# A hybrid decoder layer on one core: rows of the normed, turned input 2064 bytes apart in place of 2048

## The chip, the cores and the metric

The kernel runs on one core of one Trainium2 chip. The metric is the device time of one execution in microseconds; lower is better. The kernel before was run three times.

## What is computed

One decoder layer on 256 tokens of 1024 channels, in float32. Two token mixers (an RWKV-7 recurrence and a block-sparse attention, which at this length is plain causal attention) work on one normed input, and a gated MLP with a short convolution follows. Cut to the parts that matter here:

```python
h = rms_norm(x, norm1_g[l])
proj = h @ w_in[l]                       # 1024 -> 1824 + 1536 + 2048 columns
z_rwkv = proj[..., :RWKV_IN]
z_moba = proj[..., RWKV_IN:RWKV_IN + MOBA_IN]
gate_pre = proj[..., RWKV_IN + MOBA_IN:]
...                                      # y_a = RWKV-7 of z_rwkv, y_b = attention of z_moba
u_a = y_a @ w_branch_a[l]
u_b = y_b @ w_branch_b[l]
x = x + (g_a * u_a + g_b * u_b) @ w_out[l]
h2 = rms_norm(x, norm2_g[l])
x = x + conv_ffn(h2, w_ffn_up[l], ffn_conv_w[l], ffn_conv_b[l], w_ffn_down[l])
```

```python
u = h @ w_up                             # 1024 -> 2 * 2816
a, b = u[..., :D_FF], u[..., D_FF:]
a = causal_depthwise_conv3(a) + conv_b
return (gelu(a) * b) @ w_down
```

## The kernel before

**Numbers in two halves.** Each float32 operand of a large matmul is split into a high half, rounded to the matmul's input type (fp32r), and a low half, the rest. A product is then three matmuls: high by high, low by high, high by low. Weights come from HBM in pieces of 128 partitions by 1024 floats (`raw`); ACT makes the high half `whi` (L238) and DVE the low half `wlo` (L248). `raw` has four buffers, `whi` four, `wlo` three, all of 4096 bytes in a partition. Their refill is triggered by the matmuls that use them up, in `weights()`.

**The tile that the change touches.** `hx` holds the input of the layer's first projections, normed and turned so that channels lie on partitions: 128 partitions, 8 rows k (one for each 128 channels), and in each row the 256 tokens of the high half (`hh`) and behind them the 256 of the low half (`hl`). A row is 512 floats, 2048 bytes, and rows follow one another without a gap, so the tile is 16384 bytes in a partition. It is declared twice under one tag and has one place: first for the projections of the token mixers (L335), then again for the MLP's input (L1103).

```python
hx = cst.tile([128, 8, 2, S], F32R, name="hx", tag="hx")
hh, hl = hx[:, :, 0], hx[:, :, 1]
```

It is written row by row: ACT scales a turned piece out of PSUM into `hh[:, k]` (L393 in the first round, L1118 in the second), and DVE puts what is left into `hl[:, k]` (L396, L1119). Every read takes one row k or part of it; none spans rows.

**Who reads it.** Four places on TensorE, each an accumulation over k:

- `first` (L431) and `wst` (L278, L280, L283): weights are the stationary side, 128 columns; a half row of 256 tokens streams past. `wst` with `hx` makes the projections to r, k, v and the gates. With the outputs of the two mixers (`yah`, `yal`, `ybh`, `ybl`, each a tile of its own of four rows of 1024 bytes) the same lines make the branch projections.
- `xst` (L299, L300, L303): 128 tokens of a row of `hx` are the stationary side, and 512 columns of weights stream past; this makes q, k and v of the attention. With `mh` and `ml`, tiles of their own, the same lines make the output projection.
- `up` (L1160, L1163): weights are stationary. L1160 streams a whole row, both halves at once, 512 wide; L1163 streams the high half against `wlo`, 256 wide. The inner part is this:

```python
for m in range(2):
    ms = slice(m * 128, m * 128 + 128)
    for k in range(4):
        pe.matmul(ps_[m], wh[:, k, ms], hx[:, k0 + k].rearrange("p a s -> p (a s)"),
                  start=k0 + k == 0, stop=False, skip_group_check=True)
    for k in range(4):
        pe.matmul(ps_[m][:, 0:S], wl[:, k, ms], hh[:, k0 + k], start=False,
                  stop=k0 + k == 7, skip_group_check=True)
```

It runs for two k0 and two m, 22 times in all: 88 groups of four wide and four narrow matmuls. The down projection (L1178, L1180, L1182) streams `whi` or `wlo`, 512 wide, against the MLP's inner tile `hb`, and doesn't touch `hx`.

**The order of the work.** The first steps are in an order written by hand. From there to the branch projections, Python generators (a recurrent chain, the attention, a group norm, and `bulk` with the projections) are interleaved by costs and latencies that they hand out, and after that the code runs straight on: output projection, second norm, then eleven rounds of up projection, convolution, GELU and, one round later, down projection. Instructions keep the order in which the code issues them.

**Where tiles lie.** The pool `cst`, which holds `hx` and the constants, comes first in a partition; `hx` begins at byte 29760. The mixers' outputs and a few more tiles of `cst` follow it, then `raw`, `whi` and `wlo`, then all working tiles.

Of the kernel before, what the change touches and what calls it, by code (L numbers as in the profile page):

```python
# [9 lines left out]
F32 = mybir.dt.float32  # L10
F32R = mybir.dt.float32r
# [7 lines left out]
S = 256  # L19
# [17 lines left out]
def body(tc, x, positions, norm1_g, w_in, rwkv_mu, w_decay_up, decay_bias, w_aaa_up,  # L37
# [5 lines left out]
    with ctx:  # L43
        cst = ctx.enter_context(tc.tile_pool(name="cst", bufs=1))
# [24 lines left out]
        def acc(name="acc"):  # L69
            return ps.tile([128, 512], F32, name=name, tag="acc", bufs=3)  # L70
# [261 lines left out]
                queue += [wd[:, 2 * j - 2:2 * j - 1, :], wd[:, 2 * j - 1:2 * j, :]]  # L332
        queue += [wd[:, 20:21, :], wd[:, 21:22, :]]

        hx = cst.tile([128, 8, 2, S], F32R, name="hx", tag="hx")  # L335
        hh, hl = hx[:, :, 0], hx[:, :, 1]

        def first_steps():
# [116 lines left out]
        with tc.manual_schedule(engines={E.PE, E.Activation, E.DVE, E.Pool}):  # L455
            p = first_steps()
# [24 lines left out]
        p = acc()  # L481
# [618 lines left out]


        mh, ml = mhl
        hx = cst.tile([128, 8, 2, S], F32R, name="hx", tag="hx")  # L1103
        hh, hl = hx[:, :, 0], hx[:, :, 1]
        ss = sb.tile([128, 2, 2], F32, name="ss2")
        rs = sb.tile([128, 2], F32, name="rs2")
# [165 lines left out]
```

## Time and profile before

| what | value |
|---|---|
| median of three runs | 413.82 us (413.51 to 414.05) |
| profiled execution, span from first to last instruction | 411.9 us |
| difference between the two | 1.9 us |
| TensorE busy in the span | 404.6 us (98%) |
| VectorE (DVE), ScalarE (ACT), GpSimd (POOL) busy | 322.2, 230.8, 38.3 us |
| mean DMA rate | 172 GB/s |
| mean granted TensorE clock | 1.000 |

The profiled execution has no time of its own beside its span. PE stands for TensorE's matmuls, PEld for its weight loads. A row of a group names the line, the engine, the operation, the tile written and the tiles read, then partitions and elements. A matmul's duration runs from its first read to its modelled end in PSUM, so durations of successive matmuls overlap; the distance from start to start is shorter.

### The profile page before, as it was taken

What the parts mean: (1) busy time and instruction counts of PE and PEld (TensorE: products, weight loads), DVE (VectorE), ACT (ScalarE), POOL (GpSimd) and SP (SyncE); (2) the same over time, 40 slices, a digit from 0 to 9 for tenths busy, and PEclk for the clock granted to TensorE, in tenths of its full rate; (3) what the DMA queues carried; (4) which work ended last, traced back from release to release, by engine and by line L of the source; (5) the groups of instructions that cost most, each with busy time, mean ns of one, the idle gap of its engine ahead of it and who ended that gap; (6) DMA issues with size and microseconds to landing.
All of it is one profiled execution on the core that took longest, in us unless ns stands there. A gap on an engine that the chain in (4) does not pass through costs nothing.

```text
span 411.9 us, 8111 instructions
## 1 busy us (share of the span) xinstructions
PE 404.6 (98%) x3199; PEld 355.6 (86%) x3199; DVE 322.2 (78%) x559; ACT 230.8 (56%) x384; POOL 38.3 (9%) x62
## 2 busy tenths in 40 slices
PE   6999999999999999999999999999999999999996
PEld 3999989888899998999988888888888888888885
DVE  2888999869557876678974898979779678797784
ACT  5799645465444765453653884646446455464450
POOL 8910070000210010120000000000000000000000
PEclk9999999999999999999999999999999999999999
DMA  8955565663483352466564555765665666656612
GB/s 247 314 190 154 156 179 157 163 171 105 95 226 94 104 155 68 146 202 198 175 197 147 160 199 183 225 202 176 199 193 171 199 200 198 200 168 199 198 53 102
DMA packets 61765, 70.72 MB, mean 172 GB/s; under 512 B 8349, under 2 KB 52195, under 8 KB 61728
## 3 DMA queue, kind: packets, MB, share of 16 engines
q1 hardware_dynamic: 60768, 69.41, 56.3%
q0 software_dynamic: 944, 0.80, 0.9%
q8 instruction: 25, 0.41, 0.4%
q14 instruction: 12, 0.10, 0.1%
q10 hardware_dynamic: 16, 0.00, 0.0%
HBM read 68.76 MB, written 1.44 MB: 170 GB/s over the span
## 4 chain that ended last, share of the span: by engine, by line
PE 89%; DVE 4%; ACT 3%; DMA 1%; issue 1%; SPq 0%; POOL 0%; ACTq 0%
PE acc L1160 15%; PE acc L1163 7%; PE acc L278 7%; PE acc L283 7%; PE acc L280 7%; PE at L1160 5%; PE acc L299 5%; PE f L1182 4%; PE acc L303 4%; PE f L1180 4%; PE acc L300 4%; PE f L1178 4%; PE at L1163 2%; ACT sc L970 2%; DMA x<-in_x_dram 1%
## 5 line engine op out<-in xcount | busy, mean ns | idle before, releaser
L238 ACT CAST whi<-raw 128x1024 fp32r<-128x1024 f32 x120 | 125.8, 1051 | 113.6 <-PE acc L1160 26.2
L248 DVE TENSOR_TENSOR wlo<-raw,whi 128x1024 fp32r<-128x1024 f32 x120 | 145.7, 1218 | 41.8 <-PE acc L1163 12.9
L1160 PE MATMUL acc<-hx,whi 128*128 128x512 f32 x264 | 72.4, 395 | 0.0
L278 PE MATMUL acc<-hx,whi 128*128 128x256 f32 x232 | 58.2, 287 | 0.0
L280 PE MATMUL acc<-hx,whi 128*128 128x256 f32 x232 | 56.0, 278 | 0.0
L1160 PEld LDWEIGHTS acc<-hx,whi 128*128 128x128 f32 x264 | 45.3, 188 | 6.3
L1163 PEld LDWEIGHTS acc<-hx,wlo 128*128 128x128 f32 x264 | 40.2, 188 | 6.1
L278 PEld LDWEIGHTS acc<-hx,whi 128*128 128x128 f32 x232 | 43.6, 188 | 1.6 <-issue 0.7
L280 PEld LDWEIGHTS acc<-hx,whi 128*128 128x128 f32 x232 | 43.7, 188 | 0.1
L1163 PE MATMUL acc<-hx,wlo 128*128 128x256 f32 x264 | 41.3, 278 | 0.0
L283 PE MATMUL acc<-hx,wlo 128*128 128x256 f32 x232 | 35.9, 277 | 0.0
L1182 PE MATMUL f<-wlo,hb 128*128 128x512 f32 x80 | 31.3, 391 | 0.0
L1180 PE MATMUL f<-whi,hb 128*128 128x512 f32 x80 | 31.2, 390 | 0.0
L1178 PE MATMUL f<-whi,hb 128*128 128x512 f32 x80 | 31.2, 390 | 0.0
L283 PEld LDWEIGHTS acc<-hx,wlo 128*128 128x128 f32 x232 | 30.7, 188 | 0.3 <-issue 0.3
L1160 PE MATMUL at<-hx,whi 128*128 128x512 f32 x88 | 24.0, 394 | 0.0
L1168 DVE TENSOR_REDUCE an<-acc 128x256 f32<-128x512 f32 x22 | 15.0, 689 | 6.5 <-PE acc L1163 5.6
L299 PE MATMUL acc<-whi,hx 128*128 128x512 f32 x48 | 19.3, 403 | 0.0
L300 PE MATMUL acc<-whi,hx 128*128 128x512 f32 x48 | 18.8, 391 | 0.0
L1182 PEld LDWEIGHTS f<-wlo,hb 128*128 128x128 f32 x80 | 15.0, 188 | 3.5 <-DVE wlo L248 0.4
L1178 PEld LDWEIGHTS f<-whi,hb 128*128 128x128 f32 x80 | 15.0, 188 | 2.8
L1180 PEld LDWEIGHTS f<-whi,hb 128*128 128x128 f32 x80 | 15.0, 188 | 2.8
(311 smaller groups left out, 700.4 us busy)
## 6 DMA issues: line engine op xcount, KB each, us to landing
raw<-in_w_ffn_up_dram SPq DMA_DIRECT2D x44, 512.0 KB, 4.3
raw<-in_w_in_dram SPq DMA_DIRECT2D x38, 512.0 KB, 4.5
raw<-in_w_ffn_down_dram SPq DMA_DIRECT2D x22, 512.0 KB, 3.3
raw<-in_w_out_dram SPq DMA_DIRECT2D x8, 512.0 KB, 4.3
x<-in_x_dram SPq DMA_DIRECT2D x8, 256.0 KB, 5.2
early<-in_w_in_dram SPq DMA_DIRECT2D x4, 512.0 KB, 9.8
raw<-in_w_branch_b_dram SPq DMA_DIRECT2D x4, 512.0 KB, 3.6
raw<-in_w_branch_a_dram SPq DMA_DIRECT2D x4, 512.0 KB, 4.1
```

The lines of the kernel that those rows point to most:

```text
L238: act.copy(hi[:, :k * c], raw[:, :k * c])
L248: eng.tensor_tensor(lo[:, :n], raw[:, :n], hi[:, :n].bitcast(F32), op=OP.subtract)
L278: pe.matmul(om, wh[:, k, ms], xh[:, k0 + k], start=k0 + k + m == 0, stop=False, skip_group_check=True)
L280: pe.matmul(om, wh[:, k, ms], xl[:, k0 + k], start=False, stop=False, skip_group_check=True)
L283: pe.matmul(om, wl[:, k, ms], xh[:, k0 + k], start=False, stop=k0 + k == nk - 1 and m == n - 1, skip_group_check=True)
L299: pe.matmul(ps_[t], xh[:, K, ts], wh[:, k], start=K == 0, stop=False)
L300: pe.matmul(ps_[t], xl[:, K, ts], wh[:, k], start=False, stop=False)
L1160: pe.matmul(ps_[m], wh[:, k, ms], hx[:, k0 + k].rearrange("p a s -> p (a s)"), start=k0 + k == 0, stop=False, skip_group_check=True)
L1163: pe.matmul(ps_[m][:, 0:S], wl[:, k, ms], hh[:, k0 + k], start=False, stop=k0 + k == 7, skip_group_check=True)
L1178: pe.matmul(fin[f], hb[:, 0, i, ts], wh[:, 0, cs], start=st, stop=False, skip_group_check=f == 3)
L1180: pe.matmul(fin[f], hb[:, 1, i, ts], wh[:, 0, cs], start=False, stop=False, skip_group_check=f == 3)
L1182: pe.matmul(fin[f], hb[:, 0, i, ts], wl[:, 0, cs], start=False, stop=False, skip_group_check=f == 3)
```

## The change

Both declarations of `hx` get rows of 516 floats in place of 512, of which the first 512 are used as before. A row is then 2064 bytes from the next, and the tile is 16512 bytes. Behind it, in the same pool, a tile of 96 floats is declared that nothing reads or writes: 384 bytes. So everything that lies behind `hx` in a partition lies 512 bytes further on. The code that uses `hh`, `hl` and `hx` is as it was.

```diff
-        hx = cst.tile([128, 8, 2, S], F32R, name="hx", tag="hx")
+        hx = cst.tile([128, 8, 2 * S + 4], F32R, name="hx", tag="hx")[:, :, 0:2 * S].rearrange("p k (a s) -> p k a s", a=2)
+        cst.tile([128, 96], F32, name="gap")
         hh, hl = hx[:, :, 0], hx[:, :, 1]
...
         mh, ml = mhl
-        hx = cst.tile([128, 8, 2, S], F32R, name="hx", tag="hx")
+        hx = cst.tile([128, 8, 2 * S + 4], F32R, name="hx", tag="hx")[:, :, 0:2 * S].rearrange("p k (a s) -> p k a s", a=2)
         hh, hl = hx[:, :, 0], hx[:, :, 1]
```

## The prediction

> **What bounds the kernel now.** I read the page first: its busy times, its chain and its costliest groups.
>
> ```profile
> span 411.9 us, 8111 instructions
> PE 404.6 (98%) x3199; PEld 355.6 (86%) x3199; DVE 322.2 (78%) x559; ACT 230.8 (56%) x384; POOL 38.3 (9%) x62
> PE 89%; DVE 4%; ACT 3%; DMA 1%; issue 1%; SPq 0%; POOL 0%; ACTq 0%
> ```
>
> TensorE is busy in 404.6 of 411.9 us and holds 89% of the chain that ended last. The profiled span is 411.9 us and the median of the runs is 413.82 us, so 1.9 us lie outside the span; I add every change of the span to 413.82. The busy time by stage says how tight that is in the long last part, the gated MLP:
>
> ```profile
> 240.00:405.00 165.00, 165.00 (x874) 141.01 (x873) 133.41 (x197) 86.60 (x123) 0.00 (x0) 1.00 0.58 179
> ```
>
> The columns are the stretch, its length, the busy time of PE, of the weight loads, of DVE, ACT and POOL, then the granted TensorE clock. PE never stops in these 165 us, the clock is 1.00 throughout, and DVE, the next busiest, has 31 us to spare. So what a matmul gains or loses here reaches the end almost in full, and no other engine is close behind.
>
> PE isn't waiting, so a change of this kind can only act on how long the matmuls themselves take. I therefore asked for the groups of instructions by shape, and then for single lines with least, median and longest duration. First the matmuls that touch the changed tile (hx) and like ones that don't:
>
> ```profile
> L1160 PE MATMUL acc<-hx,whi 128*128 128x512 f32 x264 | 72.4, 395 | 0.0
> L1160 PE MATMUL at<-hx,whi 128*128 128x512 f32 x88 | 24.0, 394 | 0.0
> L1163 PE MATMUL acc<-hx,wlo 128*128 128x256 f32 x264 | 41.3, 278 | 0.0
> L1163 PE MATMUL at<-hx,wlo 128*128 128x256 f32 x88 | 13.7, 277 | 0.0
> L1180 PE MATMUL f<-whi,hb 128*128 128x512 f32 x80 | 31.2, 390 | 0.0
> L278 PE MATMUL acc<-hx,whi 128*128 128x256 f32 x232 | 58.2, 287 | 0.0
> L280 PE MATMUL acc<-hx,whi 128*128 128x256 f32 x232 | 56.0, 278 | 0.0
> L283 PE MATMUL acc<-hx,wlo 128*128 128x256 f32 x232 | 35.9, 277 | 0.0
> L300 PE MATMUL acc<-whi,hx 128*128 128x512 f32 x48 | 18.8, 391 | 0.0
> L303 PE MATMUL acc<-wlo,hx 128*128 128x512 f32 x48 | 14.9, 393 | 0.0
> L300 PE MATMUL acc<-whi,ml 128*128 128x512 f32 x32 | 12.5, 389 | 0.0
> L303 PE MATMUL acc<-wlo,mh 128*128 128x512 f32 x32 | 9.9, 390 | 0.0
> ```
>
> Before the bar stand count and shape, behind it the busy time in us and the mean in ns. Matmuls of one shape, on a full array and at one clock, don't take one time. A 512-wide one averages 395 ns when it streams hx (L1160) and 389 or 390 ns when it streams whi against mh, ml or hb. The single lines show that this isn't scatter:
>
> ```profile
> L1160 PE MATMUL acc<-hx,whi x264: 388/394/483, 224.8 to 395.3; 128*128 128x512 f32 x132
> L1180 PE MATMUL f<-whi,hb x80: 389/389/402, 248.2 to 402.4; 128*128 128x512 f32 x80
> L1163 PE MATMUL acc<-hx,wlo x264: 276/276/364, 226.3 to 395.9; 128*128 128x256 f32 x132
> L280 PE MATMUL acc<-hx,whi x232: 276/276/286, 17.4 to 177.6; 128*128 128x256 f32 x116
> L280 PE MATMUL acc<-yal,whi x32: 281/281/281, 190.4 to 201.0; 128*128 128x256 f32 x32
> L1160 PE MATMUL at<-hx,whi x88: 388/393/398, 232.3 to 396.7; 128*128 128x512 f32 x88
> ```
>
> Least, median and longest stand behind the count. L1180 has a median equal to its least value, 389. L1160 can do 388 as well, but its median is 393 or 394, and up to 398 without a wait. The same line L280 takes 276 for most of its matmuls on hx and 281 for every one of its 32 on yal. Matmul ends are modelled in such a page, so I checked it by starts, in order of time:
>
> ```profile
> 299.14 0.39 PE L1182 MATMUL f<-wlo,hb 128*128 128x512 f32 x1
> ...
> 300.05 0.39 PE L1178 MATMUL f<-whi,hb 128*128 128x512 f32 x1
> ...
> 304.84 1.09 PE L1160 MATMUL acc<-hx,whi 128*128 128x512 f32 x4
> 305.77 0.62 PE L1163 MATMUL acc<-hx,wlo 128*128 128x256 f32 x4
> 306.23 1.09 PE L1160 MATMUL acc<-hx,whi 128*128 128x512 f32 x4
> ...
> 307.62 1.09 PE L1160 MATMUL acc<-hx,whi 128*128 128x512 f32 x4
> ```
>
> Four of the down projection's matmuls start within 300.05 - 299.14 = 0.91 us, 0.227 us each. Four of the up projection's need 305.77 - 304.84 = 0.93 us, 0.2325 each. So the excess of some 5 ns is real spacing, and it repeats: one group of four wide and four narrow matmuls takes 1.39 us (304.84 to 306.23, and again to 307.62).
>
> **The change part by part.** Every engine has the same instructions in the same order with the same waits in both programs; what differs are addresses. Row k of hx starts 16k bytes later than before, and everything allocated behind hx starts 512 bytes later (128 from the longer rows, 384 from the gap). No instruction, wait or DMA is added, removed or moved.
>
> *Everything but hx, 512 bytes on: nothing.* In the group above the second half (m = 1) reads weights 512 bytes behind those of the first (m = 0), and both halves take 1.39 us; a step of 512 bytes in one operand is already tried there.
>
> *Writes of hx: nothing.* In each of two rounds ACT writes the eight high rows and DVE reads them and writes the eight low ones, 48 accesses in all:
>
> ```profile
> L393 ACT ACTIVATE hx<-xt,par x8: 467/488/522, 9.8 to 13.3; 128x256 fp32r<-128x256 f32 x8
> L1119 DVE SCALAR_TENSOR_TENSOR hx<-xt,par,hx x8: 473/476/485, 214.5 to 227.8; 128x256 fp32r<-128x256 f32 x8
> ```
>
> Nothing covers the first eight on ACT, since the projections wait for them. Were each as much as 10 ns longer, those eight and the eight of DVE behind them would cost 0.16 us; the second round lies under the output projection's matmuls.
>
> *Reads of hx by TensorE: the whole effect.* 352 wide and 352 narrow matmuls of the up projection stream hx rows, 696 narrow ones of L278, L280 and L283 and 48 of the first block do, and 144 (L299, L300, L303) load hx as the stationary side. No row here reads an operand at a step of 16 bytes, so I bound it from both sides by rows.
>
> Most that can be won, all excess gone: up, wide, 264 x (395 - 389) + 88 x (394 - 389) = 2.0 us; up, narrow, 264 x (278 - 276) + 88 x (277 - 276) = 0.6; projections, 232 x 2 for L280, 232 x 1 for L283, and 232 x 2 taken for L278, whose mean of 287 holds waits, 1.2 together; attention inputs, 48 x 2 (L300) + 48 x 3 (L303) + 48 x 3 (L299, taken as L303) = 0.4. Sum 4.2 us, so 409.6 at the least.
>
> Most that can be lost, by the slowest that rows show without a wait: 696 narrow ones to 281, which is 3 ns more for L278 and L280 and 4 for L283, 2.3 us; 48 of the first block by 5 ns, 0.2; up, narrow, to 281, 264 x 3 + 88 x 4 = 1.1; up, wide, to 398, the same count by 3 and 4, 1.1. Sum 4.8 us, so 418.6.
>
> Which value? What is slow is not set by the pitch alone: yal is a tile of its own with rows 1024 bytes apart, and all its matmuls are slow. It looks like two streams, the moving rows and the next stationary block, that meet or miss each other, and keep that from one matmul to the next because every row begins at the same place on a grid of 512 bytes. In the up projection they meet in nearly every group. Rows that begin 4 elements later each time can't keep meeting in the same way, and can't keep missing either. For the up projection and the attention inputs, where the excess is the rule, I take half of it as gone: (2.6 + 0.4) / 2 = 1.5 us. For the projections, where 276 is the median and the excess the exception, I take gains and losses as even: 0. The forecast is 413.8 - 1.5 = 412.3 us, 410.4 as a span.
>
> **The rivals.**
>
> *Nothing changes.* The excess might depend on the order of widths, four of 512 and then four of 256, more than on rows; or what is won in the up projection is lost in the projections. For it: yal shows that 2048 is not the cause. Against it: wide matmuls on mh and ml keep 389 in the same line where hx gives 391 to 393, so the operand's place matters. It gives 413.0 to 414.6, that is, 413.8 within 0.2%, which is about what a measurement of this kernel can tell from no change.
> The Trainium skill's page "TensorE: Matmul & The Clock Gate", section "Step-by-step: what each phase is for", says that TensorE has two independent read ports and that loading the next weights takes no read bandwidth from the running matmul; by that rule places in memory couldn't matter and the time would stay 413.8. The 276 and 281 ns of one line at a full clock don't fit it without something more, so I don't give this rival the most.
>
> *Slower: the narrow matmuls lose their good phase.* The place is L278, L280 and L283, which run at 276 in long stretches as things stand. If a shift of 16 bytes at each new k throws the streams out of step, half of the 696 may go to yal's 281: 348 x 5 ns = 1.7 us, with the up projection as it is, 415.5 us. With all of them slow and the up projection worse too it is the 418.6 above. Against the forecast's gain of 1.5 us it decides from 300 more slow narrow matmuls on (1.5 us / 5 ns). For it: more matmuls are now in the good state than in the bad one, so a blind shake has more to lose. Against it: those stretches come back to 276 by themselves after every interruption. A row that starts off a larger unit of memory could also cost a part of a unit per matmul; at the same 5 ns that is the same rival.
> The Trainium skill's "SBUF — State Buffer", section "Specifications (TRN2)", gives cachelines of 16 bytes; by that a step of 16 bytes leaves every row on whole lines, which speaks against such a part. No run so far shows it.
>
> **How the numbers follow.** Forecast, a gain between 0.8 and 2.9 us, 410.9 to 413.0: chance 0.43. Nothing within 0.2%: 0.26. Slower, from 414.6 up: 0.31. The time is that of the first, 412.3. The range runs from 410.9, two thirds of the largest gain, to 416.4, somewhat over half of the largest loss; beyond it I leave some 0.05 below and 0.1 above. The signs are divided, so the range is wide; the likeliest case's own is 410.9 to 413.0.
>
> **What would show it.** In the profile of the changed kernel the same rows answer. Right: L1160 with a mean near 392 in place of 395 and L1163 near 277, the group of eight at 1.37 us in place of 1.39, L280 and L283 on hx still at 277 or 278, L1180 on hb unchanged at 390. Nothing: L1160 at 394 or 395 with a median of 393 or 394. Slower: a median of 281 for L280 and L283 on hx, or L1160 near 398. The forecast fails if the medians of L278, L280 and L283 leave 276, or if L1160 doesn't fall. It would also be wrong in its ground if time appeared anywhere but in the matmuls that read hx, such as those of L1180, or in new waits.

## The result, and the profile after

The changed kernel takes 416.83 us (median of 4 runs, 415.93 to 417.06) against 413.76 us (4 runs of the kernel before, 413.51 to 414.05). The ratio is 1.0063, with a 95% interval of 1.0049 to 1.0078: 3 us slower, where 412.3 us was forecast.

The page of the changed kernel, its span and the busy times:

```profile
span 414.0 us, 8111 instructions
PE 407.4 (98%) x3199; PEld 358.5 (87%) x3199; DVE 322.5 (78%) x559; ACT 231.0 (56%) x384; POOL 37.8 (9%) x62
```

The same number of instructions, nearly the same shares, and TensorE busy for 2.8 us more (its weight loads, PEld, for 2.9). No other engine moved by more than half a microsecond. The groups of instructions by shape say where (behind L335 a line's number is one higher than before, so L1161 is the L1160 of before):

```profile
L1161 PE MATMUL acc<-hx,whi 128*128 128x512 f32 x264 | 72.0, 394 | 0.0
L278 PE MATMUL acc<-hx,whi 128*128 128x256 f32 x232 | 59.3, 289 | 0.0
L280 PE MATMUL acc<-hx,whi 128*128 128x256 f32 x232 | 57.2, 281 | 0.0
L1164 PE MATMUL acc<-hx,wlo 128*128 128x256 f32 x264 | 42.0, 281 | 0.0
L283 PE MATMUL acc<-hx,wlo 128*128 128x256 f32 x232 | 36.5, 280 | 0.0
L1181 PE MATMUL f<-whi,hb 128*128 128x512 f32 x80 | 31.2, 390 | 0.0
L300 PE MATMUL acc<-whi,hx 128*128 128x512 f32 x48 | 18.9, 394 | 0.0
L303 PE MATMUL acc<-wlo,hx 128*128 128x512 f32 x48 | 15.1, 395 | 0.0
L1164 PE MATMUL at<-hx,wlo 128*128 128x256 f32 x88 | 14.0, 281 | 0.0
```

Every group of narrow matmuls on hx is slower: L280 went from a mean of 278 ns to 281, L283 from 277 to 280, L278 from 287 to 289, and the up projection's narrow ones (L1164) from 278 and 277 to 281. The matmuls that load hx as the stationary side went from 391 and 393 to 394 and 395. Only the wide ones of the up projection gained, 1 ns on 264. L1181, which doesn't read hx, stands at 390 as before. The single lines show that it is the typical matmul that changed, not a few:

```profile
L280 PE MATMUL acc<-hx,whi x232: 276/281/289, 16.5 to 178.7; 128*128 128x256 f32 x116
L280 PE MATMUL acc<-yal,whi x32: 281/281/281, 191.4 to 202.0; 128*128 128x256 f32 x32
```

The median of L280 on hx was 276 and is 281, the value that yal had all along. By the means the sum is 232 x (2 + 3 + 3) = 1.9 us in the projections, 48 x (3 + 2) for L300 and L303, 0.2 us, and in the up projection 264 x 3 + 88 x 4 - 264 x 1 = 0.9 us: 3.0 us, nearly all of the measured loss (the first block and L299, whose means hold waits, are left out). The span grew by only 2.1 us, since the profiled execution of the changed kernel is the fastest of its four, 415.93 us. The first matmul on hx (L431, L432 now) starts at 10.3 us in the profile of before and at 9.4 in the one after, a moment that varies from run to run (9.2 us in proj_only and 9.9 in gap_only, below); from there to the start of the last matmul on hx the two differ by 3.1 us. Starts, unlike ends, aren't modelled, and they tell the parts apart: the projections' stretch went from 167.8 to 169.7 us, the MLP's up projections, with what runs between them, from 172.4 to 173.6, and the 46.7 us between the two stayed.

### The profile page after: what moved, and what is told of

The parts are those of the page before. It is cut to its first block, busy times and chain, and to the rows that moved or that the text cites. A ratio compares the mean times of both kernels' runs of the same rounds, so it can differ in the third digit from the quotient of the medians.

```text
span 414.0 us, 8111 instructions
## 1 busy us (share of the span) xinstructions
PE 407.4 (98%) x3199; PEld 358.5 (87%) x3199; DVE 322.5 (78%) x559; ACT 231.0 (56%) x384; POOL 37.8 (9%) x62
## 4 chain that ended last, share of the span: by engine, by line
PE 89%; DVE 4%; DMA 2%; ACT 2%; issue 1%; SPq 0%; ACTq 0%
PE acc L1161 12%; PE acc L278 9%; PE acc L283 8%; PE acc L280 8%; PE acc L1164 6%; PE acc L299 5%; PE acc L303 4%; PE acc L300 4%; PE f L1183 4%; PE f L1181 4%; PE f L1179 4%; PE at L1161 4%; PE at L1164 2%; DVE wlo L248 2%; DMA raw<-in_w_ffn_up_dram 1%; DMA x<-in_x_dram 1%
## 5 line engine op out<-in xcount | busy, mean ns | idle before, releaser
L1161 PE MATMUL acc<-hx,whi 128*128 128x512 f32 x264 | 72.0, 394 | 0.0
L278 PE MATMUL acc<-hx,whi 128*128 128x256 f32 x232 | 59.3, 289 | 0.0
L280 PE MATMUL acc<-hx,whi 128*128 128x256 f32 x232 | 57.2, 281 | 0.0
L1161 PEld LDWEIGHTS acc<-hx,whi 128*128 128x128 f32 x264 | 45.3, 188 | 6.2
L1164 PEld LDWEIGHTS acc<-hx,wlo 128*128 128x128 f32 x264 | 40.4, 188 | 5.9
L278 PEld LDWEIGHTS acc<-hx,whi 128*128 128x128 f32 x232 | 43.7, 188 | 1.6 <-issue 0.7
L280 PEld LDWEIGHTS acc<-hx,whi 128*128 128x128 f32 x232 | 43.7, 188 | 0.1
L1164 PE MATMUL acc<-hx,wlo 128*128 128x256 f32 x264 | 42.0, 281 | 0.0
L283 PE MATMUL acc<-hx,wlo 128*128 128x256 f32 x232 | 36.5, 280 | 0.0
L283 PEld LDWEIGHTS acc<-hx,wlo 128*128 128x128 f32 x232 | 31.2, 188 | 0.3 <-issue 0.3
L1181 PE MATMUL f<-whi,hb 128*128 128x512 f32 x80 | 31.2, 390 | 0.0
L1161 PE MATMUL at<-hx,whi 128*128 128x512 f32 x88 | 24.0, 394 | 0.0
L299 PE MATMUL acc<-whi,hx 128*128 128x512 f32 x48 | 19.4, 405 | 0.0
L300 PE MATMUL acc<-whi,hx 128*128 128x512 f32 x48 | 18.9, 394 | 0.0
L1181 PEld LDWEIGHTS f<-whi,hb 128*128 128x128 f32 x80 | 15.0, 188 | 2.9
```

Source lines behind the costliest of these rows:

```text
L278: pe.matmul(om, wh[:, k, ms], xh[:, k0 + k], start=k0 + k + m == 0, stop=False, skip_group_check=True)
L280: pe.matmul(om, wh[:, k, ms], xl[:, k0 + k], start=False, stop=False, skip_group_check=True)
L283: pe.matmul(om, wl[:, k, ms], xh[:, k0 + k], start=False, stop=k0 + k == nk - 1 and m == n - 1, skip_group_check=True)
L299: pe.matmul(ps_[t], xh[:, K, ts], wh[:, k], start=K == 0, stop=False)
L300: pe.matmul(ps_[t], xl[:, K, ts], wh[:, k], start=False, stop=False)
L1181: pe.matmul(fin[f], hb[:, 1, i, ts], wh[:, 0, cs], start=False, stop=False, skip_group_check=f == 3)
```

## The experiments

After the result there were three theories. *Step*: rows that begin 16 bytes later from one k to the next throw two streams of reads out of step. *Start*: a row that begins off some grid costs by itself. *Neighbours*: what costs is that everything behind hx moved by 512 bytes. In all variants of the layer that follow, but for a repeat of the changed kernel, hx is a flat tile of 4224 floats, so that everything behind it lies where it lies in the changed kernel; only the rows' pitch and first place differ. Each ratio is to the kernel before, run beside the variant.

**gap_only: pitch 2048, first row at 0.**

```diff
-        hx = cst.tile([128, 8, 2, S], F32R, name="hx", tag="hx")
+        hx = cst.tile([128, 4224], F32R, name="hx", tag="hx")[:, 0:4096].rearrange("p (k r) -> p k r", k=8)[:, :, 0:512].rearrange("p k (a s) -> p k a s", a=2)
```

> Rows stay 2048 bytes apart; 512 bytes of gap stand behind them, so that everything else lies where it lies in the changed kernel. Theory 'step' (rows that begin 16 bytes later from one k to the next put the narrow matmuls out of step) and theory 'start' (a row that begins off the old grid costs by itself, wherever the row before it began): 413.8 us, L278, L280 and L283 on hx with a median of 276 ns. Theory 'neighbours' (the 512 bytes by which whi, wlo and the rest move are what costs): 416.8 us and a median of 280 ns.

Measured 413.29 us, ratio 0.9988 (0.9971 to 1.0004), the median of L280 on hx 276 ns. The neighbours are out.

**shift16: pitch 2048, every row 16 bytes later.**

```diff
-...[:, 0:4096]...
+...[:, 4:4100]...
```

> Rows stay 2048 bytes apart, but all of them begin 16 bytes later; the rest lies as in the changed kernel. Theory 'step': all rows are alike again, so the narrow matmuls can lock into one state; 413.8 us within 1 us, a narrow median that is one value and not a mixture. Theory 'start': every row begins off the old grid, in place of six of eight; 417 to 418 us and narrow matmuls at 280 ns or more. Theory 'neighbours': 416.8.

Measured 417.24 us, ratio 1.0065 (1.0042 to 1.0089): as slow as the change, though no row is shifted against the next.

```profile
L280 PE MATMUL acc<-hx,whi x232: 278/281/288, 16.5 to 179.0; 128*128 128x256 f32 x116
```

This is against *step* and for *start*: not one of these 232 matmuls reaches 276, and none of L278 and L283 does.

**step64: pitch 2112, a step of 64 bytes.**

```diff
-...[:, 0:4096].rearrange("p (k r) -> p k r", k=8)...
+...[:, 0:4224].rearrange("p (k r) -> p k r", k=8)...
```

> Rows 2112 bytes apart, a step of 64 bytes; the rest lies as in the changed kernel. Theory 'step' leaves the size of the grid open: if the streams repeat every 64 bytes, 413.8 us and a narrow median of 276; if the grid is larger (128 to 512 bytes), 416 to 417 us as with 16 bytes. Theory 'start', with a grid of 64 bytes: 413.8 us. Theory 'neighbours': 416.8.

Measured 414.84 us, ratio 1.0016 (1.0001 to 1.0031), and the projections are nearly as slow as in the changed kernel:

```profile
L280 PE MATMUL acc<-hx,whi x232: 274/280/288, 17.2 to 178.8; 128*128 128x256 f32 x116
```

The wide matmuls of the up projection gained (393 ns in place of 395), which gives part of it back. That is against *start* with a grid of 64 bytes. Both theories had one run against them, so I formed a third, *place*: what counts is how far a moving row stands from the stationary block that is loaded beside it, on a grid larger than 64 bytes. *Step* became *lock*: rows that all begin alike, at a multiple of 64 bytes, settle into a fast order wherever they stand.

**proj_only and mlp_only: the long rows for one part alone.** The first declaration has rows of 516 floats and the second of 512, or the other way round.

```diff
-        hx = ...[:, 0:4096].rearrange("p (k r) -> p k r", k=8)...
+        hx = ...[:, 0:4128].rearrange("p (k r) -> p k r", k=8)...
```

> Rows 2064 bytes apart for the projections of the mixers, 2048 for the MLP. By the profile of the changed kernel (narrow means of the projections 2 to 3 ns up on 696 matmuls, starts some 4 ns further apart, attention inputs 3 ns up on 144) most of the loss is here: theories 'step' and 'start' 416.2 us, that is 2.4 of the 3.0 us. If the MLP's part is the larger, 414.5 us or less. Theory 'neighbours': 416.8.

> Rows 2048 bytes apart for the projections of the mixers, 2064 for the MLP; everything else lies as in the changed kernel. If the parts add up: the changed kernel's +3.0 us less the +1.2 us measured with the long rows in the projections alone, 415.8 us. By spacings alone (narrow +3.2 ns on 352, wide -1.2 ns on 352) +0.7 us, 414.6.

Measured 415.33 us, ratio 1.0028 (1.0013 to 1.0042), and 414.56 us, 1.0001 (0.9986 to 1.0015). Together, 0.0029, they fell short of the whole, 0.0063, and the projections alone were expected at 416.2 us. So both were run again beside the changed kernel on one chip, as proj_again, mlp_again and after_again; only the name of the gap tile differs.

> The changed kernel once more, beside its two parts on one chip. All theories: a ratio of 1.006 to the kernel before, 416.5 us.

> Rows 2064 bytes apart for the projections alone, once more. If the parts add up: with the next run, the sum of the two gains in the ratio equals that of the changed kernel, 0.006; I expect 0.004 here. If the first measurement stands: 0.003.

> Rows 2064 bytes apart for the MLP alone, once more. If the parts add up: 0.002 in the ratio, 414.7 us. If the first measurement stands: 0.000, and the sum of the parts falls short of the whole.

Measured 415.92 us, ratio 1.006 (1.0037 to 1.0084), for the whole; 415.02 us, 1.0038 (1.0026 to 1.005), for the projections; 414.31 us, 1.0017 (1.0001 to 1.0032), for the MLP. The parts add up to 1.0055 of 1.006. Two thirds of the loss are in the projections of the mixers with the attention inputs, as the sum of the means has it.

The profile of mlp_only shows something else. Its projections have the rows of gap_only, at the same place, and mlp_again is the same program; yet the median of L278 is 281 ns in the one and 276 in the other (L280 and L283: 277 and 276).

```profile
L278 PE MATMUL acc<-hx,whi x232: 275/281/470, 16.2 to 177.3; 128*128 128x256 f32 x116
```

So the place alone doesn't fix the time: one layout ran at two paces.

**micro: the streams alone.** The layer is left out; x is copied to the output. TensorE runs blocks of matmuls in the projections' and in the up projection's order on one tile X of rows, and no other engine has work beside them.

```diff
+        for nm, off in OFFS:            # rows 2048 bytes apart, first row at off
+            spacer(3)
+            narrow(nm, off, 0)
+        for nm, step in STEPS:          # first row at 64 bytes, a step beyond 2048
+            spacer(3)
+            narrow(nm, 16, step)
```

> Leaves the layer out: it runs only streams of matmuls and copies x to the output. Blocks of 48 narrow matmuls in the projections' order, and blocks of 32 wide and 32 narrow in the up projection's order, on one tile of rows; eleven blocks with rows 2048 bytes apart that begin 0, 16, 32, 48, 64, 128, 192, 256, 320, 384 or 448 bytes into the tile, and six blocks that begin at 64 with steps of 16, 32, 64, 128, 256 and 512 bytes beyond 2048. No other engine works beside them. Theory 'place' (the spacing follows from where a row begins against the next stationary block): blocks at constant offsets differ, 113.3 to 120 ns for narrow ones, and a block with a step has the mean of the offsets that its rows pass. Theory 'lock' (rows that all begin alike let the streams settle into a fast order, whatever the offset, if it is a multiple of 64 bytes): all offsets that are multiples of 64 give 113 to 114 ns, 16, 32 and 48 some 117 to 119, and every step 117 or more, above the mean of its offsets, but for 512. A theory that other engines' reads and writes cause the excess: 113.3 ns for narrow and 226.7 for wide in all blocks.

A narrow block has 96 matmuls, not the 48 that were announced. X and the weights' tile W begin at the same place of a 256-byte grid, so the offset is the distance. Four of the blocks, by tile: narrow_a has its rows at 0, narrow_f at 128, narrow_h at 256 and narrow_l at 448 bytes.

```profile
L90 PE MATMUL narrow_a<-X,W x32: 280/283/283, 30.2 to 54.6; 128*128 128x256 f32 x32
L90 PE MATMUL narrow_f<-X,W x32: 279/281/285, 97.8 to 108.1; 128*128 128x256 f32 x32
L90 PE MATMUL narrow_h<-X,W x32: 283/283/283, 120.5 to 131.0; 128*128 128x256 f32 x32
L90 PE MATMUL narrow_l<-X,W x32: 276/276/276, 154.7 to 164.6; 128*128 128x256 f32 x32
```

With nothing else running, the same matmul takes 276, 281 or 283 ns by the place of its rows. Offsets 0 and 256 give the same 283; 128 and 384 give 281 on average; the odd multiples of 64 give a mean of either 276 (448) or 279 to 281 (64, 192, 320); 16, 32 and 48 give 279 to 281. Every block with a step, from 16 to 512 bytes, has a mean of 279 to 281. So *lock* is wrong, since 0, 128 and 256 are multiples of 64 and slow, and other engines aren't needed for it. *Place* holds, with one addition: at the odd multiples of 64 two steady states are possible.

The blocks in the up projection's order, four wide and four narrow in turn (named mixed), bear on the other half of the forecast. Their wide matmuls have means of 393 to 399 ns and medians of 392 to 397 at all eleven offsets and all six steps. No place brings them to the 389 to 391 of the down projection in the kernel before, whose matmuls are wide throughout.

**shift64: pitch 2048, every row 64 bytes later.**

```diff
-...[:, 0:4096]...
+...[:, 16:4112]...
```

> Rows stay 2048 bytes apart, but all begin 64 bytes later, so that they stand to 128 bytes as the weights' tiles do; everything else lies as in the changed kernel. Theory 'start' with a grid of 64 bytes and theory 'lock': 413.5 us, narrow median 276. Theory 'place': the rows then stand to the weights as whi to hb in the kernel's last matmuls, where wide ones are spaced 227 ns and narrow ones 120 ns: up projection wide 352 x -5 ns, narrow 352 x +5, projections 744 x +5.5, together +4 us, 417 to 418.

In the kernel before, hx stands 192 bytes from whi and wlo on the grid of 256; here the distance is 0. Measured 416.88 us, ratio 1.0066 (1.0045 to 1.0087), with these lines:

```profile
L280 PE MATMUL acc<-hx,whi x232: 277/283/288, 16.5 to 179.3; 128*128 128x256 f32 x116
L300 PE MATMUL acc<-whi,hx x48: 388/390/398, 46.4 to 110.8; 128*128 128x512 f32 x48
```

Narrow matmuls went to 283, as *place* had it from the kernel's last ones, and the wide ones that load hx went the other way, from a median of 392 to 390. *Start* and *lock* wanted 276 and 413.5 us. By the ratio that is 2.7 us more than the kernel before, where 4 were expected. It isn't that the wide matmuls gained more: those of the up projection kept their excess, with means of 394 and 395 where 5 ns less was expected. In the profiles, the time from the first matmul on hx to the start of the last grew by the 4.0 us expected (9.4 to 400.3 us against 10.3 to 397.2); the first came 0.9 us earlier, and whether that makes up the rest is not shown.

**micro2: whose place, and what is met.** The same blocks, with the weights moved too, and with stationary blocks of 64 and 32 columns.

```diff
-                        pe.matmul(o, W[:, 0, k, ms], r(k0 + k)[:, 0:256], ...)
+                        pe.matmul(o, w(0, k, m), r(k0 + k)[:, 0:256], ...)      # W from w0 on, cols columns
```

> Leaves the layer out, as the first stream kernel did: blocks of 48 narrow matmuls in the projections' order, rows 2048 bytes apart, now with the weights' tile moved too (0 to 256 bytes), and with stationary blocks of 64 and of 32 columns in place of 128. Theory 'place', in the form that the first stream kernel left (what counts is the distance from the moving row to the next stationary block, on a grid of 256 bytes): equal moves of both give what no move gave, 119.7 ns (both by 16, 64, 128 or 192 bytes); weights moved by 64 or 192 alone give the states 113.3 or 117.8, by 128 alone 118.6, by 256 alone 119.7, by 16 alone 117 to 119. If it is the meeting of two reads, blocks of 32 columns, which are read in a quarter of the time, lose most of the excess and most of the difference between rows' places: 109 to 114 ns whatever the place. Theory 'row' (the place of the moving row alone counts): moving the weights changes nothing, 119.7 with rows at 0, 117.8 or 113.3 at 64, 118.6 at 128; and the columns of the stationary block change nothing.

Rows and weights: both 64 bytes later (narrow_e), weights alone by 128 (narrow_b), weights alone by 64 (narrow_a).

```profile
L95 PE MATMUL narrow_e<-X,W x32: 281/283/283, 80.5 to 90.9; 128*128 128x256 f32 x32
L95 PE MATMUL narrow_b<-X,W x32: 279/281/287, 28.2 to 57.2; 128*128 128x256 f32 x32
L95 PE MATMUL narrow_a<-X,W x32: 276/276/285, 25.9 to 49.1; 128*128 128x256 f32 x32
```

Moving both by 64 gives the 283 of no move; moving the weights alone does what moving the rows alone did. Block narrow_a was issued in turns with its neighbours, and its two other lines have a median of 278, so it holds both states. So the distance counts, and theory *row* is out. One pair doesn't fit: both moved by 16 gave 277 to 281 and not 283, so below 64 bytes the place itself plays a part too. Then 32 columns, with rows at 0, 16, 64 and 128 bytes (narrow_p, q, r, s, of which the first two are shown), and 64 columns at 0 (narrow_l):

```profile
L92 PE MATMUL narrow_p<-X,W x32: 276/276/280, 192.5 to 202.7; 128*32 128x256 f32 x32
L92 PE MATMUL narrow_q<-X,W x32: 275/275/282, 203.4 to 213.6; 128*32 128x256 f32 x32
L92 PE MATMUL narrow_l<-X,W x32: 276/276/279, 148.0 to 158.2; 128*64 128x256 f32 x32
```

With a quarter of the columns to load, all four places give 275 or 276, the 16-byte one too; a weight load takes 108 ns there in place of 188 to 192, not a quarter of the time. With 64 columns (134 ns a load) the place still matters, but otherwise: 0, the slowest place for 128 columns, gives 276, and 16, 64 and 128 give means of 277 to 280. What is shown is that the excess hangs on the distance of the two operands and on the size of the stationary block together. That the moving row's read meets the read of the next block is the simplest reading of it, and is not shown by itself: a profile shows loads and matmuls but not their reads from memory, all blocks in these runs lie alike on the grid, so that the next can't be told from the present one, and a smaller block also writes fewer partitions of PSUM.

## Why the prediction was wrong

**What bounds the kernel** was right: TensorE, without waits in the last part, so that some nanoseconds per matmul reach the end.

**Neighbours and writes at nothing** was right: 0.9988 (0.9971 to 1.0004) with the neighbours moved alone. The writes of hx stand unchanged in the rows of ACT (467/488/510 ns after, 467/488/522 before).

**That places in memory decide** was right, and micro and micro2 show it; two streams that meet or miss are the reading that fits. One of its two grounds was luck, though. The tiles of the mixers' outputs lie behind hx at whole multiples of 256 bytes, so yal stands at the same 192 bytes as hx: its 281 ns against 276 is not another place but the other pace, as in mlp_only; ybl, laid alike, has a median of 276 on the same line. The grid is 256 bytes and not 512 (offsets 0 and 256 give 283). The rule of the Trainium skill's page "TensorE: Matmul & The Clock Gate", section "Step-by-step: what each phase is for", that loading the next weights takes no read bandwidth from the running matmul, differs from these runs: 276 against 283 ns by the distance of the two operands, and 275 or 276 at every place with a block of 32 columns. The measurement decides.

**The step that failed** is this one: "For the projections, where 276 is the median and the excess the exception, I take gains and losses as even: 0." The median was the warning. With 128 columns only one kind of distance, the odd multiples of 64 bytes, has a steady state of 276, the kernel before stands on it with 192 bytes, and every other place tried in micro, and every step, gives a mean of 279 to 283. So there was little to gain and much to lose: 1.9 us by the means, ratio 1.0038 measured for this part and the attention inputs together. The place, the lines and the end value of 281 are those of the rival on the slower side. Its price of 1.7 us was for half of the 696 matmuls at 5 ns; in fact the typical one is affected, and the mean of all rose by 2 to 3 ns. So that price came close, by a count and a size that were both off.

**Half of the excess gone in the up projection and the attention inputs** failed in size and sign. The wide matmuls gained 1 ns on 264, 0.3 us, where 1 us was forecast (half of 2.0); the narrow ones lost 3 to 4 ns on 352, 1.1 us, where 0.3 us of gain was forecast; L300 and L303 lost 0.2 us. The MLP's part alone measured 1.0017. The excess of the wide ones was taken for a matter of place, of which a shake must remove half. But it is there at every place and step of micro's mixed blocks, and at 0 bytes in shift64 (394 and 395 ns); that points to the order of widths, as the rival *Nothing changes* had allowed for, though no run changed the order alone. The narrow ones do follow the place: with rows of 2064 bytes eight distances from 192 to 304 take turns, and of these only 192 is an odd multiple of 64.

**The range** ended at 416.4 us, 0.4 below the measured median: its upper end was somewhat over half of the largest loss, and the projections and the narrow matmuls of the up projection lost together.

**The remark on memory lines** (the Trainium skill's "SBUF — State Buffer", section "Specifications (TRN2)", cachelines of 16 bytes) pointed the wrong way: whole lines are no protection, as shift16 with 417.24 us shows. What matters here repeats after 256 bytes, 283 ns at 0 and at 256.

What stays open: what selects between the two states at an odd multiple of 64 bytes. Rows at 192 bytes gave about 281 in micro and 276 in all four blocks of micro2 that had the same place, 276 for most of hx and 281 for yal in one kernel, and both for hx in two runs of one program. So part of what the change lost hangs on a pace that the layout before permits and doesn't guarantee. And no variant shows a layout that beats the kernel before; the nearest, gap_only, isn't told apart from it.

## What to carry to other kernels

When a matmul streams against a freshly loaded stationary block, compare the least, median and longest duration of one line on different tiles before blaming a pitch. A spread of 5 ns at full clock doesn't yet say why: hx and yal stood at one distance. Move one operand alone, by 16, 64 and 128 bytes, before trusting a cause. Where the median already equals the least value, an edit to the layout has little to win, so price it at the slow value for all of them, not for half. And ask whether the excess is there at other places too, before counting half of it as won. Keep the size of every tile ahead of the operands in mind: an edit that looks unrelated can move the distance between the operands.

## What the runs showed of the hardware

- A 256-wide fp32r matmul on a full array takes about 276, 281 or 283 ns (mean starts 0.113 to 0.120 us apart, in micro and micro2) by the distance between its moving row and the stationary blocks, modulo 256 bytes: 283 at 0, 281 at 128, 276 or 279 to 281 at the odd multiples of 64, and 277 to 282 in the mean off the 64-byte grid.
- At 192 bytes both 276 and 281 are met in one program: hx against yal in the kernel before, and L278 on hx in mlp_only (281) against mlp_again (276).
- A stationary block of 32 columns in place of 128 removes this dependence: 275 or 276 ns at all four places tried in micro2. With 64 columns 0 is the best place tried, with 276.
- Wide matmuls rank the distances differently: those that load hx have a median of 390 ns at distance 0 (shift64) and of 392 at 192 bytes (before), while the narrow ones have 283 and 276. In the up projection's order no place tried brings wide ones below a mean of 393 ns (micro).
